# Block 0's weight split, the row splits and the last norm in the output projection of a hybrid layer

## The chip, the cores and the metric

The kernel runs on one core of a Trainium2 chip. The metric is the device time of one execution in microseconds (us). The engines are TensorE (PE, with PEld for its weight loads), VectorE (DVE), ScalarE (ACT), GpSimd (POOL) and SyncE (SP, which here only issues DMA transfers). Each engine works through its own instruction queue; semaphores order them against each other.

## The reference, cut to what matters

One layer of a diffusion backbone on 1024 latent tokens and 256 context tokens of width 1024, all in fp32:

```python
y_m = mlstm_merge(hm, om, mlstm_norm[l])               # 4 heads x 128, chunkwise mLSTM
y_a = window_attention(q, k, v, k_ctx, v_ctx, sink)    # 8 query / 2 kv heads x 64, |i-j| <= 128
x = x + g_a * (jnp.concatenate([y_m, y_a], axis=-1) @ w_out[l])
h = modulate(rmsnorm(x, norm_ffn[l]), sh_f, sc_f)
a, val = jnp.split(h @ w_up[l], 2, axis=-1)            # w_up: 1024 x 5632
x = x + g_f * ((gelu(dwconv(a, conv_w, conv_b)) * val) @ w_down[l])
return rmsnorm(x, final_norm)
```

## The kernel before, in words

Every fp32 matrix product is made of three products of fp32r halves: a value is split into a high half (a rounding copy) and a low half (value minus high half), and hi*hi, hi*lo and lo*hi are accumulated (`mm3`, lines 307 to 309). So each operand costs one cast and one subtraction before PE can use it; each product costs three PE instructions.

The stage that the change touches lies between attention and the up-projection. The tokens are eight tiles of 128 rows.

*Attention* (`Pair`, loop over `t`) runs 32 pairs of heads as a software pipeline: scores (`S`), row maximum, exponential (`ex`), scaling on POOL (`nrm`), transposes (`tr`), their splits (`hi` on ACT, `lo` on DVE), products with v (`pv`) into one PSUM tile `u` and the write of the result into `yTa` (`y1`, `y2`). `fill(t, i)` inserts other work at fixed places of a step: the mLSTM half of the output projection (`Wout(b, 0)`), the whole projection of tile 0 (`f0`), and row splits (`ysplit_h`, `ysplit_l`) of attention's result for the first tiles of the next loop. Steps are numbered up to n + 1, with n = 32.

*Output projection* (the loop over `order` = 4, 1, 5, 2, 6, 3, 7, from line 1471 on). For each tile b: two groups of twelve products (`wout_n(b, 0)`, `wout_n(b, 1)`) into two PSUM buffers (`po`), each added to the rows `xs[b]` on DVE (line 1374); sums of squares on ACT (`sq`); the norm factor (root on ACT, reciprocal on DVE) and the normed rows `hn` on ACT (`norm_b`); eight transposes on PE (`trans`); evacuation with scale and shift, four parts on ACT and four on DVE (`evac`, L1417 and L1419); and splits into `hB` (`split`, L1430 and L1192). These follow one another over three turns of the loop, so a turn works on the products of tile b, the norm of the tile before and the evacuation of the one before that.

*The up-projection is a Strassen product.* Tokens are two halves (tiles 0 to 3 and 4 to 7), so `hB` holds seven operands: B11, B21, B22 and the sums T1 to T4, which need both tiles of a pair (b - 4 and b; `sum1` to `sum4`). The weights come in pairs `Ra`, `Rb` with four sums (`sums_v`, `sums_g`) and splits (`wsplit`). Block 0's first product uses the weights `er`, split into `e0`. Its products a (with e0) start before the last tile is ready, on 384 of 512 columns; then come the groups f, c, b, e and d, and then block 1.

*What sets the order.* Attention and the loop over `order` are each written in a hand-ordered section (`manual_schedule`): PE, DVE, ACT and POOL take their instructions in program order there. What stands between or behind these sections (the split of `e0` at line 1349, the sums and splits from line 1571 on) and SP's queue are placed by the framework's planner. `held` is a list of postponed subtractions that `run` empties.

Of the kernel before, what the change touches and what calls it, by code (L numbers as in the profile page):

```python
# [9 lines left out]
F32 = mybir.dt.float32  # L10
F32R = mybir.dt.float32r
# [7 lines left out]
P = 128  # L19
# [59 lines left out]
def build(tc, I, out, dbg=None):  # L79
# [959 lines left out]


    p2 = ExitStack()
    yp = p2.enter_context(tc.tile_pool(name="yp", bufs=1))
    yTa = yp.tile([P, 4, SEQ], F32, name="yTa")
    wop = p2.enter_context(tc.tile_pool(name="wop", bufs=1))
    pb_ = ExitStack()
    t3 = pb_.enter_context(tc.tile_pool(name="t3", bufs=2, reuse_waits="tile"))
# [8 lines left out]
    class Wout:  # L1055
# [15 lines left out]
        def hi(self):  # L1071
            self.h, self.l = (t2.tile([P, 512], F32R, name=n, tag=n, bufs=1) for n in ("ymh", "yml"))
            r = lambda a: a[:].rearrange("p (j q) -> p j q", j=4)
            self.src = yTa[:, :, self.b * P:self.b * P + P] if self.attn else r(self.po)
            S.copy(r(self.h), self.src)

        def lo(self):
# [16 lines left out]
    class Pair:  # L1094
# [87 lines left out]

        def y2(self):
            u, ut = self.u, self.ut
            yf = yTa[:, 2 * self.g + self.r, self.b * P:(self.b + 1) * P]
            V.tensor_tensor(out=yf[0:64], in0=u[0:64, 0:P], in1=ut[0:64], op=ALU.add)
            V.tensor_tensor(out=yf[64:128], in0=u[64:128, P:2 * P], in1=ut[64:128], op=ALU.add)

    order = [4, 1, 5, 2, 6, 3, 7]
    ys = {}  # L1190
    yslice = lambda b: yTa[:, :, b * P:(b + 1) * P]
    sub = lambda e, o, x, y: e.tensor_tensor(out=o, in0=x, in1=y, op=ALU.subtract)  # L1192

    def ysplit_h(b, eng=G):
        ys[b] = [t4.tile([P, 4, P], F32R, name=f"y{n}", tag=f"y{n}", bufs=3 if n == "h" else 2) for n in "hl"]
        eng.copy(ys[b][0][:], yslice(b)) if eng is S else eng.tensor_copy(ys[b][0][:], yslice(b))

    def ysplit_l(b):
        sub(V, ys[b][1][:], yslice(b), ys[b][0][:].bitcast(F32))

    pairs = [(b, g, r) for b in range(NL) for g in range(KVH) for r in range(2)]
    pSs = [(pk, "pp")]
# [40 lines left out]
    more[n - 4, 0] += [f0.load]  # L1243
    more[n - 3, 2] += [f0.hi, f0.lo]
    tail_of(f0, n - 2)
    more[n - 5, 0] += [lambda: ysplit_h(order[0], S)]
    more[n - 5, 2] += [lambda: ysplit_l(order[0])]
    more[n - 4, 0] += [lambda: ysplit_h(order[1], S)]
    more[n - 3, 0] += [lambda: ysplit_l(order[1])]
    more[n - 2, 0] += [lambda: ysplit_h(order[2], S)]  # L1250

    attn = tc.manual_schedule(engines={mybir.EngineType.PE, mybir.EngineType.DVE, mybir.EngineType.Activation,
                                       mybir.EngineType.Pool})
# [86 lines left out]
    def split2(hi, lo, src):  # L1340
        S.copy(hi, src)
        V.tensor_tensor(out=lo, in0=src, in1=hi.bitcast(F32), op=ALU.subtract)  # L1342

    er = eW.tile([P, 2, 512], F32, name="er")
    e0 = [eW.tile([P, 2, 512], F32R, name=f"e0{n}") for n in "hl"]
    ar0 = eW.tile([P, 512], F32, name="ar0")
    a0 = [eW.tile([P, 512], F32R, name=f"a0{n}") for n in "hl"]
    nc.sync.dma_start(er[:], I["w_up"][0, :, 0:2].rearrange("p q k f -> p q (k f)"))
    split2(e0[0][:], e0[1][:], er[:])
    flat = lambda a: a[:].rearrange("p a b -> p (a b)")  # L1350

    pu = ExitStack()
# [9 lines left out]
    def load_x(b):  # L1362
        xs[b] = t3.tile([P, D], F32, name="x2", tag="x2")[:]
        nc.sync.dma_start(xs[b], x2_d[b][:])

    def wout_n(b, n, mid=None):
        ns = slice(512 * n, 512 * n + 512)
        po = pO.tile([P, 512], F32, name="po", tag="o")
        yh, yl = ys[b]
        for kt in range(4):  # L1370
            if kt == 2 and mid:
                mid()
            mm3(po[:], yh[:, kt], yl[:, kt], wos[4 + kt][0][:, ns], wos[4 + kt][1][:, ns], kt == 0, kt == 3)
        return lambda: V.tensor_tensor(out=xs[b][:, ns], in0=po[:], in1=xs[b][:, ns], op=ALU.add)

    def sq(b, n):
        if n == 0:
            hns[b] = t5.tile([P, D], F32, name="hn", tag="hn")
            rs[b] = t5.tile([P, 3], F32, name="r2", tag="r2")
        ns = slice(512 * n, 512 * n + 512)  # L1380
        S.activation(hns[b][:, ns], xs[b][:, ns], AF.Square, accum_out=rs[b][:, n:n + 1])
        if n == 1:
            run(1)
            V.tensor_scalar(out=rs[b][:, 2:3], in0=rs[b][:, 0:1], scalar1=1.0 / D, scalar2=EPS, op0=ALU.mult, op1=ALU.add)
            S.activation(rs[b][:, 0:1], rs[b][:, 1:2], AF.Sqrt, bias=rs[b][:, 2:3], scale=1.0 / D)
# [49 lines left out]
        sub(V, raws[b - 4][:, 0], raws[b][:, 0], raws[b - 4][:, 0])  # L1435

    def sum2(b):
        tbs[b] = tbp.tile([P, 1, 4, P], F32, name="tb", tag="tb", bufs=1)
        sub(V, tbs[b][:, 0], raws[b][:, 1], raws[b - 4][:, 0])

    def sum3(b, e=V):
# [13 lines left out]
    def prod(ps, wt, j, blk, first, last, by_part=None, cols=slice(0, 512), kts=range(4)):  # L1455
        seq = [(kt, p_) for p_ in by_part for kt in kts] if by_part else [(kt, p_) for kt in kts for p_ in parts]
        for n, (kt, (sw, part)) in enumerate(seq):
            T.matmul(ps[:, cols], wt[sw][:, j, kt * P:kt * P + P], hB[part][:, blk, kt, cols],  # L1458
                     start=first and n == 0, stop=last and n == len(seq) - 1,
                     skip_group_check=not first and len(kts) == 4)  # L1460

    load_x(order[0])
    fence = tc.manual_schedule(engines={mybir.EngineType.PE, mybir.EngineType.DVE, mybir.EngineType.Activation,
                                        mybir.EngineType.Pool})
# [6 lines left out]
    for i, b in enumerate(order):  # L1471
        prev = order[i - 1] if i else None
        pp = order[i - 2] if i > 1 else 0 if i == 1 else None
        add0 = wout_n(b, 0)
        if prev is not None:
            sq(prev, 1)
            norm_b(prev)
        run()
        if pp is not None:
            evac(pp)  # L1480
        if 0 < i and i + 2 < len(order):
            ysplit_h(order[i + 2])
        if 0 < i and i + 1 < len(order):
            ysplit_l(order[i + 1])
        if pp is not None and pp >= 4:
            held.append(split_b(pp))
        add0()
        sq(b, 0)
        if pp is not None and pp < 4:
            held.append(split(pp, B11, 2, raws[pp][:], V))  # L1490
            if late is not None:
                held.append(split_t3(late))
                held.append(split_t4(late))
            late = None
            run(1)
        if pp is not None and pp >= 4:
            sum1(pp)
            sum2(pp)
            held.append(split_t1(pp))
            held.append(split_t2(pp))  # L1500
            run(2)
            held += [lambda a=pp: sum3(a), lambda a=pp: sum4(a)]
            late = pp
        if b != last:
            add1 = wout_n(b, 1)
            trans(prev if i else 0)
            add1()
            nc.sync.dma_start(x2_d[b][:], xs[b])
# [12 lines left out]
    prod(ps_a2, e0, 1, B21, True, False, None, c3, range(2))
    trans(last, (4, 5, 6, 7))
    prod(ps_a2, e0, 1, B21, False, True, None, c3, range(2, 4))
    trans(last, (0, 1, 2, 3))
    prod(ps_a, e0, 0, B11, True, True, None, c1)
# [5 lines left out]
    p2.close()  # L1531


    f = ExitStack()
    fr = f.enter_context(tc.tile_pool(name="fr", bufs=1, reuse_waits="tile"))
    fw = f.enter_context(tc.tile_pool(name="fw", bufs=5, reuse_waits="tile"))
    add = lambda e, o, x, y: e.tensor_tensor(out=o, in0=x, in1=y, op=ALU.add)


    def load_R(m, ts=(0, 1), R=None):  # L1540
        R = R or [fr.tile([P, 2 + 3 * t, 512], F32, name=f"R{'ab'[t]}", tag=f"R{t}") if t in ts else None for t in range(2)]
        for t in ts:
            R[t] = R[t] or fr.tile([P, 2 + 3 * t, 512], F32, name=f"R{'ab'[t]}", tag=f"R{t}")
            nc.sync.dma_start(R[t][:, 0:2], I["w_up"][m, :, 2 * t:2 * t + 2].rearrange("p q k f -> p q (k f)"))
        return R

    def sums_v(R, e=V):
        add(e, R[1][:, 2], R[1][:, 1], R[1][:, 0])
        sub(e, R[1][:, 3], R[1][:, 2], R[0][:, 0])


    def sums_g(R, e=V):
        sub(e, R[1][:, 4], R[0][:, 1], R[1][:, 3])
        sub(e, R[1][:, 1], R[0][:, 0], R[1][:, 1])

    def wsplit(R, n):
        return wsplit_h(R, n)()

# [9 lines left out]
        return lo  # L1568


    R = load_R(0)
    sums_v(R)
    evac(last, range(4, 8))
    sub(V, R[1][:, 4], R[0][:, 1], R[1][:, 3])
    lo_b = split_b(last)
    wB = wsplit_h(R, 3)
    evac(last, range(4))
    lo_b()
    wB = wB()
    sum1(last)  # L1580
    wS = wsplit_h(R, 1)
    lo_1 = split_t1(last)
    S.copy(ar0[:], ps_a[:])
    run()
    wS = wS()
    sum2(last)
    lo_1()
    sub(V, R[1][:, 1], R[0][:, 0], R[1][:, 1])
    lo_2 = split_t2(last)
    lo_2()  # L1590
    lo_3, lo_4 = split_t3(late), split_t4(late)
    wA = wsplit_h(R, 2)
    lo_3()
    sum3(last)
    wA = wA()
    lo_5 = split_t3(last)
    lo_5()
    lo_4()
    sum4(last)
    split_t4(last)()  # L1600
    pTk.close()
    pC = pu.enter_context(tc.tile_pool(name="pC", bufs=4, space=PSUM, side="right", reuse_waits="tile"))
# [120 lines left out]
    for i in range(1, NF):  # L1723
# [416 lines left out]
```

## Time and profile before

| | us |
|---|---|
| median of 3 runs (lowest, highest) | 1275.53 (1273.96, 1277.4) |
| the profiled execution | 1275.56 |
| its span | 1273.7 |
| PE busy in the span | 1239.2 |
| DVE busy | 972.1 |
| ACT busy | 639.5 |
| POOL busy | 187.5 |

The span runs from the first to the last instruction of the trace; 1.9 us lie around it. Times inside the trace count from the start of the span. A row of a timeline gives start, duration, engine, line of the kernel, operation, output and inputs; in brackets stands how long the engine had been idle and what ended that. `wh`, `wl` are weight halves, `yh`, `yl` the halves of attention's result, `x` the rows, `hn` the normed rows.

### The profile page before, as it was taken

The page shows a single profiled execution, that of the slowest core. Times are in us where ns is not written, and L with a number is a line of the kernel's source. Part 1 is how long each engine was busy: PE and PEld are TensorE (multiplying, and loading weights), DVE is VectorE, ACT ScalarE, POOL GpSimd, SP SyncE. Part 2 cuts the span into 40 slices and gives each one's busy share as a digit, 9 for nine tenths or more (in the row PEclk, how much of TensorE's full clock was granted, in tenths as well). Part 3 has the DMA queues.
Part 4 walks back from the last instruction along what each step waited for, and adds up shares of the span by engine and source line. Part 5 has one row for each costly group of instructions (what it writes and reads, how often), then busy time and mean ns, then how long its engine had stood idle before and what let it go on. Part 6 is the DMA issues. An engine that isn't in the chain of part 4 may idle for free.

```text
span 1273.7 us, 19249 instructions
## 1 busy us (share of the span) xinstructions
PE 1239.2 (97%) x7047; PEld 1062.8 (83%) x7047; DVE 972.1 (76%) x1689; ACT 639.5 (50%) x1311; POOL 187.5 (15%) x162
## 2 busy tenths in 40 slices
PE   6999999999999999999899999999999999999997
PEld 4799998999898888888788888888888888788886
DVE  4863687878787888786997877777777776867887
ACT  6732556464865777776844333333333333434435
POOL 1200000000001444221002321232231232001000
PEclk9999999999999999999999999999999999999999
DMA  9531444462355332112423322233322337975553
GB/s 357 184 125 35 142 130 144 117 177 84 84 174 160 131 111 89 62 39 102 156 74 111 120 100 92 108 108 108 108 99 91 108 117 268 344 255 179 193 197 134
DMA packets 90416, 175.64 MB, mean 138 GB/s; under 512 B 12938, under 2 KB 29522, under 8 KB 90322
## 3 DMA queue, kind: packets, MB, share of 16 engines
q1 hardware_dynamic: 90034, 173.63, 40.4%
q8 instruction: 56, 0.92, 0.3%
q10 hardware_dynamic: 288, 0.79, 0.2%
q14 instruction: 38, 0.31, 0.1%
HBM read 136.05 MB, written 38.33 MB: 137 GB/s over the span
## 4 chain that ended last, share of the span: by engine, by line
PE 81%; DVE 7%; DMA 4%; ACT 4%; issue 2%; SPq 1%; POOL 1%; ACTq 0%; DVEq 0%; POOLq 0%
PE pd L1979 14%; PE pa L1458 9%; PE pc L1458 9%; PE pp L588 7%; PE pe L1458 5%; PE pb L1458 4%; PE pd L1458 4%; PE u L1175 3%; PE pt L1152 2%; PE pv L307 2%; PE pv L309 2%; PE pv L308 2%; PE po L307 2%; PE po L308 1%; PE po L309 1%
## 5 line engine op out<-in xcount | busy, mean ns | idle before, releaser
L1563 ACT CAST wh<-Rb 128x1024 fp32r<-128x1024 f32 (+1 forms) x66 | 59.5, 904 | 143.5 <-PE pd L1458 77.1
L1979 PE MATMUL pd<-dh,al 128*128 128x512 f32 x296 | 115.4, 390 | 0.7 <-DVE al L1342 0.6
L1979 PE MATMUL pd<-dl,ah 128*128 128x512 f32 x296 | 115.2, 389 | 0.0
L1979 PE MATMUL pd<-dh,ah 128*128 128x512 f32 x296 | 115.2, 389 | 0.0
L1458 PE MATMUL pc<-hB,wh 128*128 128x512 f32 x344 | 105.6, 389 | 0.0
L1458 PE MATMUL pa<-hB,wh 128*128 128x512 f32 x336 | 103.7, 390 | 0.2 <-ACT sn L1641 0.2
L1192 DVE TENSOR_TENSOR wl<-Rb,wh 128x1024 fp32r<-128x1024 f32 (+1 forms) x66 | 68.9, 1045 | 39.2 <-ACT wh L1563 38.6
L1677 POOL TENSOR_TENSOR tt<-vt,tt 128x512 f32<-128x512 f32 x22 | 29.5, 1340 | 349.0 <-ACT tt L1671 349.0
L588 PE MATMUL pp<-hl,wh 128*128 128x512 f32 x256 | 79.4, 405 | 0.0
L307 PE MATMUL pv<-wh,hl 128*128 128x256 f32 x256 | 76.0, 297 | 0.5 <-ACT ym L601 0.5
L1458 PEld LDWEIGHTS pc<-hB,wh 128*128 128x128 f32 x344 | 64.5, 188 | 13.5
L1458 PEld LDWEIGHTS pa<-hB,wh 128*128 128x128 f32 x336 | 62.9, 188 | 14.1 <-ACT sn L1641 1.1
L309 PE MATMUL pv<-wh,hl 128*128 128x256 f32 x256 | 72.3, 283 | 0.0
L308 PE MATMUL pv<-wl,hl 128*128 128x256 f32 x256 | 72.3, 282 | 0.0
L1458 PE MATMUL pc<-hB,wl 128*128 128x512 f32 x172 | 66.4, 389 | 0.0
L1979 PEld LDWEIGHTS pd<-dh,al 128*128 128x128 f32 x296 | 55.5, 188 | 12.8 <-DVE al L1342 1.4
L1979 PEld LDWEIGHTS pd<-dl,ah 128*128 128x128 f32 x296 | 55.6, 188 | 11.9 <-DVE dl L1342 0.2
L1458 PE MATMUL pa<-hB,wl 128*128 128x512 f32 x168 | 65.4, 389 | 0.0
L1979 PEld LDWEIGHTS pd<-dh,ah 128*128 128x128 f32 x296 | 55.6, 188 | 11.6
L1159 ACT CAST ph<-pt 128x512 fp32r<-128x512 f32 (+1 forms) x88 | 46.2, 525 | 27.6 <-PE pt L1152 27.4
L1458 PE MATMUL pe<-hB,wh 128*128 128x512 f32 x176 | 54.4, 390 | 0.0
L1458 PE MATMUL pb<-hB,wh 128*128 128x512 f32 x176 | 54.2, 389 | 0.0
(1065 smaller groups left out, 3695.5 us busy)
## 6 DMA issues: line engine op xcount, KB each, us to landing
w<-in_w_ada_dram SPq DMA_DIRECT2D x64, 256.0 KB, 2.7
br<-in_w_down_dram SPq DMA_DIRECT2D x25, 512.0 KB, 5.5
Ra<-in_w_up_dram SPq DMA_DIRECT2D x22, 512.0 KB, 3.6
Rb<-in_w_up_dram SPq DMA_DIRECT2D x22, 512.0 KB, 3.5
ar<-act_s SPq DMA_DIRECT2D x44, 256.0 KB, 3.0
act_a<-tt SPq DMA_DIRECT2D x33, 256.0 KB, 2.0
act_s<-tt SPq DMA_DIRECT2D x33, 256.0 KB, 2.0
wr<-in_w_h_dram SPq DMA_DIRECT2D x16, 512.0 KB, 4.4
```

The costliest lines, as they stand in the source:

```text
L307: T.matmul(ps, st_hi, mv_hi, start=first, stop=False)
L308: T.matmul(ps, st_hi, mv_lo, start=False, stop=False)
L309: T.matmul(ps, st_lo, mv_hi, start=False, stop=last)
L588: T.matmul(pp[:, 512 * n:512 * n + 512], wkq[sw][:, kt, cs], hl[n][part][:, kt, :], start=kt == 0 and sw + part == 0, stop=kt == KT - 1 an ...
L1152: T.transpose(self.pt[i][:, (2 * kk + j) * P:(2 * kk + j + 1) * P], self.p[j][:, kb * P:(kb + 1) * P], ident[:])
L1159: S.copy(self.ph[i][:, :w], self.pt[i][:, :w])
L1175: T.matmul(self.u[:], vv[:, c, self.g], part[i][:, kk * 2 * P:(kk + 1) * 2 * P], start=kb + m == 0, stop=kb == last and m == 1)
L1192: sub = lambda e, o, x, y: e.tensor_tensor(out=o, in0=x, in1=y, op=ALU.subtract)
L1458: T.matmul(ps[:, cols], wt[sw][:, j, kt * P:kt * P + P], hB[part][:, blk, kt, cols], start=first and n == 0, stop=last and n == len(seq) - ...
L1563: S.copy(wt[0][:], src)
L1677: G.tensor_tensor(out=self.tt[:, h2_], in0=self.vt[:], in1=self.tt[:, h2_], op=ALU.mult)
L1979: T.matmul(ps[:], ac[sa][:, js], w[sw], start=first and n == 0, stop=last and n == 2, skip_group_check=not fresh)
```

## The change

Attention's result becomes three tiles instead of one (blocks 0 and 1, blocks 2 to 6, block 7), and their memory is later used for block weights: `Ra` in the first, `Rb` in the second, `ar0` in the third. The row splits of tiles 4 and 1 are placed in attention's last two steps (n and n + 1) instead of n - 5 to n - 3. The split of `e0` and the high halves of the five other tiles stand in the loop's first turn (one on ACT, four on POOL, with room in `hB` columns that only the last pair of tiles fills); their low halves stand in the first three turns. In the turns 0 and 1 the high half of an evacuated tile is cast on ACT, afterwards on DVE. The weights `Ra`, `Rb` are loaded in turn 2, two of their sums are formed in turn 4 and two in turn 6 (through `held`). Behind the loop, the squares and the norm of the last tile stand ahead of the split of tile 3, and the rest is reordered.

```diff
-    yTa = yp.tile([P, 4, SEQ], F32, name="yTa")
+    yTa = [yp.tile([P, w, 4, P], F32, name="yT", tag=f"yT{w}") for w in (2, 5, 1)]
...
-    more[n - 5, 0] += [lambda: ysplit_h(order[0], S)]
-    more[n - 5, 2] += [lambda: ysplit_l(order[0])]
-    more[n - 4, 0] += [lambda: ysplit_h(order[1], S)]
-    more[n - 3, 0] += [lambda: ysplit_l(order[1])]
-    more[n - 2, 0] += [lambda: ysplit_h(order[2], S)]
+    more[n, 0] += [lambda: ysplit_h(order[0], S)]
+    more[n, 2] += [lambda: ysplit_l(order[0])]
+    more[n + 1, 0] += [lambda: ysplit_h(order[1], S)]
+    more[n + 1, 2] += [lambda: ysplit_l(order[1])]
...
-    split2(e0[0][:], e0[1][:], er[:])
...
-        if 0 < i and i + 2 < len(order):
-            ysplit_h(order[i + 2])
-        if 0 < i and i + 1 < len(order):
-            ysplit_l(order[i + 1])
-        if pp is not None and pp >= 4:
-            held.append(split_b(pp))
         add0()
+        if i == 0:
+            split2(e0[0][:], e0[1][:], er[:])
+            for j in range(2, 7):
+                ysplit_h(order[j], S if j == 2 else G, [hB[n][:, B22 + j - 2, :, 3 * P:4 * P] for n in range(2)])
         sq(b, 0)
+        for j in ((2, 3), (4, 5), (6,))[i] if i < 3 else ():
+            ysplit_l(order[j])
+        if b == last:
+            break
         if pp is not None and pp < 4:
-            held.append(split(pp, B11, 2, raws[pp][:], V))
+            held.append(split(pp, B11, 2, raws[pp][:], V if i > 1 else S))
...
+        if i == 2:
+            R = load_R(0)
+        if i == 3:
+            held.append(lambda: sums_v(R))
+        if i == 5:
+            held.append(lambda: (sub(V, R[1][:, 4], R[0][:, 1], R[1][:, 3]), sub(V, R[1][:, 1], R[0][:, 0], R[1][:, 1])))
...
     add1 = wout_n(last, 1, lambda: trans(prev))
     evac(prev)
     add1()
+    sum1(late)
+    sum2(late)
+    sq(last, 1)
+    lo_b = split_b(late)
+    norm_b(last, True)
     lo3 = split(prev, B11, 2, raws[prev][:])
-    sq(last, 1)
-    norm_b(last, True)
-    lo3()
+    lo_b()
     prod(ps_a, e0, 0, B11, True, True, None, c3)
     prod(ps_a2, e0, 1, B21, True, False, None, c3, range(2))
     trans(last, (4, 5, 6, 7))
+    evac(last, range(4, 8))
+    lo3()
...
-    R = load_R(0)
-    sums_v(R)
```

## Rows read from the trace of the kernel before

**Rows 1.** The page's first part: engine, busy us, share of the span, instructions.
```profile
PE 1239.2 (97%) x7047; PEld 1062.8 (83%) x7047; DVE 972.1 (76%) x1689; ACT 639.5 (50%) x1311; POOL 187.5 (15%) x162
```

**Rows 2.** Busy time by stage: stretch, length, engines (instructions), PE clock, DMA share, GB/s.
```profile
564.00:567.00 3.00, 1.42 (x9) 1.16 (x9) 1.88 (x4) 2.41 (x6) 0.20 (x1) 0.99 0.41 165
567.00:574.00 7.00, 6.79 (x26) 5.79 (x25) 4.46 (x10) 4.25 (x12) 1.80 (x3) 0.52 0.00 0
574.00:583.60 9.60, 9.16 (x59) 7.75 (x58) 5.02 (x10) 3.39 (x8) 0.93 (x2) 1.00 0.01 2
583.60:600.00 16.40, 16.40 (x83) 13.75 (x82) 9.97 (x25) 12.65 (x29) 1.54 (x2) 1.00 0.46 162
...
618.00:635.10 17.10, 14.09 (x71) 11.43 (x70) 16.04 (x36) 14.41 (x33) 0.00 (x0) 1.00 0.45 154
635.10:654.40 19.30, 18.55 (x98) 15.67 (x99) 18.24 (x30) 10.32 (x17) 0.00 (x0) 1.00 0.23 83
```

**Rows 3.** Timeline of the end of attention, PE, ACT and DVE.
```profile
564.55 0.47 PE L1175 MATMUL u<-ph,vv 128*128 128x256 f32 x2 [0.56 <-ACT p__7262 L1133]
...
564.86 0.40 PE L1175 MATMUL u<-pl__7266,vv 128*128 128x256 f32 x2
565.13 1.04 ACT L1341 CAST e0h<-er 128x1024 fp32r<-128x1024 f32 x1 [0.59 <-DMA er<-in_w_up_dram]
...
566.29 0.39 PE L1118 MATMUL sps<-kT,QT 128*128 128x256 f32 x1 [1.03 <-ACT sps L1109]
...
567.33 0.79 PE L1175 MATMUL u<-ph,vv 128*128 128x256 f32 x2 [0.21 <-ACT ph L1159]
```

**Rows 4.** Timeline of PE up to the first product of the output projection.
```profile
573.19 0.63 PE L308 MATMUL po<-wol,ymh 128*128 128x512 f32 x1
...
574.85 0.27 PE L1152 MATMUL pt<-ident,p__7262 128*128 128x128 f32 x1
...
583.62 0.39 PE L307 MATMUL po<-woh,yh 128*128 128x512 f32 x1
```

**Rows 5.** Timeline of PE in the output projection: instructions that follow a wait.
```profile
622.84 0.47 PE L307 MATMUL po<-woh,yh 128*128 128x512 f32 x1 [0.59 <-DVE x L1374]
...
627.72 1.09 PE L1406 MATMUL pt<-ident,hn 128*128 128x128 f32 x8 [0.52 <-ACT hn L1394]
...
635.85 0.66 PE L1406 MATMUL pt<-ident,hn 128*128 128x128 f32 x4 [2.52 <-DVE hn L1392]
```

**Rows 6.** Timeline of DVE in the output projection: tile 4's additions, one later turn.
```profile
587.60 0.69 DVE L1374 TENSOR_TENSOR x<-po,x 128x512 f32<-128x512 f32 x1
589.29 0.69 DVE L1374 TENSOR_TENSOR x<-po,x 128x512 f32<-128x512 f32 x1 [1.00 <-PE po L309]
...
622.01 0.68 DVE L1374 TENSOR_TENSOR x<-po,x 128x512 f32<-128x512 f32 x1
622.61 0.68 DVE L1430 CAST hB<-raw 128x1024 fp32r<-128x1024 f32 x1
623.32 1.22 DVE L1192 TENSOR_TENSOR hB<-raw,hB 128x1024 fp32r<-128x1024 f32 x1
624.47 0.68 DVE L1374 TENSOR_TENSOR x<-po,x 128x512 f32<-128x512 f32 x1
```

**Rows 7.** Timeline of ACT in the output projection: norm, evacuation, casts.
```profile
591.30 1.15 ACT L1394 ACTIVATE hn<-x,r 128x1024 f32<-128x1024 f32 x1 [0.23 <-DVE r L1389]
592.35 1.48 ACT L1417 ACTIVATE raw<-pt,ada 128x128 f32<-128x128 f32 x4
...
623.35 1.13 ACT L1430 CAST hB<-raw 128x512 fp32r<-128x512 f32 x2
```

**Rows 8.** POOL's casts of yh: ns shortest/median/longest, first and last start, forms.
```profile
L1196 POOL CAST yh<-yTa x4: 610/771/1106, 589.1 to 608.1; 128x512 fp32r<-128x512 f32 x4
```

**Rows 9.** The page's DMA issues: KB each, median us to landing.
```profile
Rb<-in_w_up_dram SPq DMA_DIRECT2D x22, 512.0 KB, 3.5
```

**Rows 10.** Timeline of DVE: the last norm's reciprocal and the last low half of T3.
```profile
635.11 0.16 DVE L1389 RECIPROCAL r<-r 128x1 f32<-128x1 f32 x1 [0.26 <-ACT r L1385]
...
648.35 0.68 DVE L1192 TENSOR_TENSOR hB<-er,hB 128x512 fp32r<-128x512 f32 x1
```

**Rows 11.** Timeline of PE: start of group f, and of block 1 behind group d.
```profile
640.46 2.04 PE L1458 MATMUL pf<-hB,wh 128*128 128x512 f32 x8
...
654.44 0.62 PE L1458 MATMUL pa<-hB,wh 128*128 128x512 f32 x2
```

More of the change, by code (lines that the diff above doesn't have):

```diff
@@ L1041, in build @@
     p2 = ExitStack()
-    yp = p2.enter_context(tc.tile_pool(name="yp", bufs=1))
-    yTa = yp.tile([P, 4, SEQ], F32, name="yTa")
+    yk = ExitStack()
+    yp = yk.enter_context(tc.tile_pool(name="yp", bufs=1))
+    yTa = [yp.tile([P, w, 4, P], F32, name="yT", tag=f"yT{w}") for w in (2, 5, 1)]
+    yslice = lambda b: yTa[0][:, b] if b < 2 else yTa[1][:, b - 2] if b < 7 else yTa[2][:, 0]
     wop = p2.enter_context(tc.tile_pool(name="wop", bufs=1))
@@ L1073, in hi @@
             r = lambda a: a[:].rearrange("p (j q) -> p j q", j=4)
-            self.src = yTa[:, :, self.b * P:self.b * P + P] if self.attn else r(self.po)
+            self.src = yslice(self.b) if self.attn else r(self.po)
             S.copy(r(self.h), self.src)
@@ L1184, in y2 @@
             u, ut = self.u, self.ut
-            yf = yTa[:, 2 * self.g + self.r, self.b * P:(self.b + 1) * P]
+            yf = yslice(self.b)[:, 2 * self.g + self.r]
             V.tensor_tensor(out=yf[0:64], in0=u[0:64, 0:P], in1=ut[0:64], op=ALU.add)
@@ L1190, in build, with ysplit_h @@
     ys = {}
-    yslice = lambda b: yTa[:, :, b * P:(b + 1) * P]
     sub = lambda e, o, x, y: e.tensor_tensor(out=o, in0=x, in1=y, op=ALU.subtract)
-    def ysplit_h(b, eng=G):
-        ys[b] = [t4.tile([P, 4, P], F32R, name=f"y{n}", tag=f"y{n}", bufs=3 if n == "h" else 2) for n in "hl"]
-        eng.copy(ys[b][0][:], yslice(b)) if eng is S else eng.tensor_copy(ys[b][0][:], yslice(b))
+    def ysplit_h(b, eng=G, room=None):
+        ys[b] = room or [t4.tile([P, 4, P], F32R, name=f"y{n}", tag=f"y{n}")[:] for n in "hl"]
+        eng.copy(ys[b][0], yslice(b)) if eng is S else eng.tensor_copy(ys[b][0], yslice(b))
     def ysplit_l(b):
-        sub(V, ys[b][1][:], yslice(b), ys[b][0][:].bitcast(F32))
+        sub(V, ys[b][1], yslice(b), ys[b][0].bitcast(F32))
     pairs = [(b, g, r) for b in range(NL) for g in range(KVH) for r in range(2)]
@@ L1345, in build @@
     e0 = [eW.tile([P, 2, 512], F32R, name=f"e0{n}") for n in "hl"]
-    ar0 = eW.tile([P, 512], F32, name="ar0")
     a0 = [eW.tile([P, 512], F32R, name=f"a0{n}") for n in "hl"]
     nc.sync.dma_start(er[:], I["w_up"][0, :, 0:2].rearrange("p q k f -> p q (k f)"))
-    split2(e0[0][:], e0[1][:], er[:])
     flat = lambda a: a[:].rearrange("p a b -> p (a b)")
@@ L1370, in wout_n @@
         for kt in range(4):
-            if kt == 2 and mid:
+            if kt == 3 and mid:
                 mid()
@@ L1437, in sum2 @@
     def sum2(b):
-        tbs[b] = tbp.tile([P, 1, 4, P], F32, name="tb", tag="tb", bufs=1)
+        tbs[b] = tbp.tile([P, 1, 4, P], F32, name="tb", tag="tb", bufs=2)
         sub(V, tbs[b][:, 0], raws[b][:, 1], raws[b - 4][:, 0])
@@ L1460, in prod, with load_R, sums_v, sums_g @@
                      skip_group_check=not first and len(kts) == 4)
+    add = lambda e, o, x, y: e.tensor_tensor(out=o, in0=x, in1=y, op=ALU.add)
+    def load_R(m, ts=(0, 1), R=None):
+        R = R or [None, None]
+        for t in ts:
+            R[t] = yp.tile([P, 2 + 3 * t, 512], F32, name=f"R{'ab'[t]}", tag=f"yT{2 + 3 * t}")
+            nc.sync.dma_start(R[t][:, 0:2], I["w_up"][m, :, 2 * t:2 * t + 2].rearrange("p q k f -> p q (k f)"))
+        return R
+    def sums_v(R, e=V):
+        add(e, R[1][:, 2], R[1][:, 1], R[1][:, 0])
+        sub(e, R[1][:, 3], R[1][:, 2], R[0][:, 0])
+    def sums_g(R, e=V):
+        sub(e, R[1][:, 4], R[0][:, 1], R[1][:, 3])
+        sub(e, R[1][:, 1], R[0][:, 0], R[1][:, 1])
     load_x(order[0])
@@ L1496, in build @@
         if pp is not None and pp >= 4:
+            held.append(split_b(pp))
             sum1(pp)
@@ L1503, in build @@
             late = pp
[L1504 to L1508, printed above, removed]
+        add1 = wout_n(b, 1)
+        trans(prev if i else 0)
+        add1()
+        nc.sync.dma_start(x2_d[b][:], xs[b])
         if i + 2 < len(order):
             load_x(order[i + 2])
+        if i == 2:
[4 more added lines that the diff above has]
+            held.append(lambda: (sub(V, R[1][:, 4], R[0][:, 1], R[1][:, 3]), sub(V, R[1][:, 1], R[0][:, 0], R[1][:, 1])))
+    late = pp
     ps_a, ps_a2 = (pA.tile([P, 512], F32, name="pa", tag="a") for _ in range(2))
@@ L1531, in build @@
     p2.close()
+    ar0 = yp.tile([P, 512], F32, name="ar0", tag="yT1")
     f = ExitStack()
-    fr = f.enter_context(tc.tile_pool(name="fr", bufs=1, reuse_waits="tile"))
     fw = f.enter_context(tc.tile_pool(name="fw", bufs=5, reuse_waits="tile"))
[L1537 to L1554, printed above, removed]
     def wsplit(R, n):
@@ L1568, in wsplit_h @@
         return lo
-    R = load_R(0)
-    sums_v(R)
-    evac(last, range(4, 8))
-    sub(V, R[1][:, 4], R[0][:, 1], R[1][:, 3])
     lo_b = split_b(last)
     wB = wsplit_h(R, 3)
+    lo_1 = split_t1(late)
     evac(last, range(4))
@@ L1579, in build @@
     wB = wB()
+    lo_1()
+    wS = wsplit_h(R, 1)
+    lo_2 = split_t2(late)
     sum1(last)
-    wS = wsplit_h(R, 1)
     lo_1 = split_t1(last)
-    S.copy(ar0[:], ps_a[:])
-    run()
     wS = wS()
+    lo_1()
+    lo_2()
+    sum4(late)
     sum2(last)
-    lo_1()
-    sub(V, R[1][:, 1], R[0][:, 0], R[1][:, 1])
     lo_2 = split_t2(last)
+    sum3(late)
     lo_2()
     lo_3, lo_4 = split_t3(late), split_t4(late)
+    S.copy(ar0[:], ps_a[:])
     wA = wsplit_h(R, 2)
+    sum3(last)
     lo_3()
-    sum3(last)
     wA = wA()
     lo_5 = split_t3(last)
+    sum4(last)
     lo_5()
     lo_4()
-    sum4(last)
     split_t4(last)()
@@ L1799, in build @@
     f.close()
+    yk.close()
     g = ExitStack()
```

## The prediction

> **What bounds the kernel now.** I read the page first: TensorE (PE) is busy 97% of the span [rows 1], so a change pays only where PE waits or runs at its lower clock. The table by stage then finds both around the edit [rows 2]. [...] In the output projection PE is full up to 618 and busy 14.09 of 17.10 us from there to 635.1, where VectorE (DVE) is busy 16.04: that end is paced by DVE. At its start (583.6 to 600) DVE is busy only 9.97 of 16.4. From 635.1 to 654.4 PE loses 0.75 more. All that this change could take back is therefore some 2 us of waits and 3.3 of low clock in attention's end, and 3.8 us (3.01 + 0.75) in and behind the projection.
>
> The timeline shows why. At 565.13 ScalarE (ACT), after 0.59 of idling for the load of er, casts e0h for 1.04; the sink copy that the next scores wait for stands behind it, and PE idles 1.03 [rows 3]. It had idled 0.56 before and idles 0.21 after, then the clock falls. A 512-column product then takes 0.63 where it takes 0.39 later [rows 4], start to start 0.43 against 0.23.
>
> Below, T is the time since the projection's first product, which stands at 583.62 in the trace [rows 4].
>
> **End of attention: e0 and the three early row splits leave.** Without e0h the sink copy follows the exponential at once, and the scores can start behind the product of 564.86 [rows 3], at 565.2. From there to the transposes of 574.85 [rows 4], PE's work at full clock is two score groups 1.15 (four products of 256 columns and a short one each), twelve products of 256 columns 1.4 (half of 0.23 each), eight transposes 0.9 (eight in 1.09, [rows 5]), six products of 512 columns 1.4: 4.8 us. DVE and ACT, laid out beside it, make PE wait about 0.45 for one low half (pl). So 574.85 comes at about 570.5, 4.3 us earlier. The wait of 0.56 at 564.55 stays: it ends with the pair before leaving its single PSUM buffer. The splits of tiles 4 and 1 return two pairs later, on ACT and DVE, which are busy 3.39 and 5.02 of the 9.6 us there [rows 2]. The cast holds back one ph cast by 0.52, which DVE's addition of po covers; without that cover it costs 0.5. Ends of this term: 1.2 us (waits of 1.03 and 0.21 go, the clock falls all the same) and 5.4 (the 0.56 and the 0.45 go as well). I take 4.3, since a busy PE at full clock is what both neighbouring rows of the table show.
>
> **Output projection, first three tiles.** Start to start, DVE needs 0.60 for 512 columns, 1.15 for a two-input 1024, 0.71 for a 1024 cast [rows 6]; ACT 1.05 for a norm, 1.4 for its half of an evacuation, 0.5 for a 512 cast (two in 1.13) [rows 7], 0.95 for a 1024 cast (1.04 long, [rows 3]). Both queues keep the written order. The norm of tile 0 starts on ACT at T 3.98, unchanged: its chain hangs on the end of attention. Behind it stand now e0h (T 5.0 to 6.1) and the high half of tile 5 (to 6.6). On DVE the first addition of tile 4 still starts at T 3.98 (587.60, [rows 6]); then e0l waits for e0h until 6.14, and with the low halves of tiles 5 and 2 DVE is engaged until 8.5. So tile 4's second addition starts at T 8.5, not at 5.67 (589.29, [rows 6]): 2.8 us later. PE does not feel it yet: the PSUM buffer that this frees is wanted at T 9.2, when it comes free.
>
> In tile 1 the whole chain behind that addition (square, root, norm, evacuation) is late by as much; the low halves of tiles 6 and 3 fill DVE, and the cast of tile 0's rows, now ACT's, ends at 14.6. DVE waits 1.2 for it, and the second addition starts at 15.8, not 12.2. PE wants that buffer at 15.7 and gets it at 16.6: 0.9 of waiting. From tile 2 on DVE no longer has low halves beyond one, nor the slowing by POOL's casts, which took between 0.61 and 1.11 us beside it [rows 8]; all four are now issued together behind attention, while DVE is mostly idle. The second additions come at T 22.9, 29.5, 37.2, 43.8 and 50.1; in the trace the last one is at 49.3. PE waits another 0.6, 0.1, 0.9 and 0.2 for buffers, which replaces the 0.59 [rows 5] and its like.
>
> **Weight sums.** Four DVE operations of 0.6 to 0.7 (2.5 us) move from behind the last norm into tiles 6 and 7. Their loads go on SP behind tile 6's rows, at about T 26, and land by T 30.6 at 3.5 us [rows 9] plus issue and rivalry with the row loads; the sums want them at T 31.4. Late by 1 us they stall DVE by 0.2, by 2 us 1.2. In exchange, five 0.6 operations of tile 6's sums and splits go behind the norm.
>
> **The last norm.** Its reciprocal comes at T 52.5, against 51.5 [rows 10]. PE, idle since 52.0, gets the transposes at T 53.2 (trace: 52.2 [rows 5]), so its idle shrinks from 2.52 to about 1.25. But the 1024 cast of tile 3's rows now stands behind the norm on ACT (to 54.6), its low half on DVE ends at T 55.9, and the products on the last 128 columns need it: they wait 0.85 and end at T 58.6, where the trace has 56.8 (640.46, [rows 11]). From the norm on, DVE must do 14.1 us of operations up to the last low half of T3, with 1.4 of waits for ACT, against 13.84 in all before (635.11 to 648.35 and 0.60 for that operation itself, [rows 10]). The fourth product group (e) wants that half at T 67.1 and gets it at 68.2: about 1.2 us. The five groups end at T 73.5; the trace has T 70.8 (654.44, [rows 11]). From there on PE is full before, and block 1's weights are ready 3 us before they are due.
>
> **The rest** costs nothing: the R tiles lie in y's memory, e0 and ar0 have other places, and all are free long before their next writer (covered by whole tiles of PE work; if not, a load of 3.5 is exposed).
>
> **Sum.** 4.3 earlier, 2.7 later: 1.6 us gained. The profiled execution took 1275.56 us for a span of 1273.7, the median is 1275.53; so 1274.0. The projection's term lies between -3.8 (all of PE's idle there goes) and +4.7 (the 2.8 of tile 4 is never caught up, and the 1.9 of the late products is added).
>
> **Rivals.** *The projection keeps pace:* DVE's idle at the start really takes the low halves, and the queue walk overrates ACT's holds. For it: DVE has 6.4 us idle there [rows 2]. Against: those low halves now stand behind an ACT cast that stands behind the norm. Then 4.3 remains and up to 3.8 is added: 1267.5 to 1271.2, middle 1269.5.
>
> *The low clock was not e0's:* the split goes, but the granted clock falls at the end of attention as before, since the 0.56 of idling and the short products stay. Then 1.2 is gained and 2.7 lost: 1277.0. Against: of the 1.80 us of idling that came ahead of the fall [rows 3], 0.56 is left.
>
> *The other side, slower:* the clock falls in the projection. PE now waits in nearly every tile for one of two PSUM buffers, and twice between transposes around the last norm. If it is granted half for a stretch like that of 567 to 574, this costs 3.3 us (6.79 of work at 0.48 less): 1277.3, and 1280.6 if it happens in tile 1 and again behind the norm; it decides from 1.6 us of lost work on. Against: after idling 2.52 us at 635.85 [rows 5] the clock stayed at 1.00 [rows 2]. [...] The trace's 0.59 wait on such a buffer, without a fall, speaks against it.
>
> **How the numbers follow.** About 0.3%, 3.8 us, is what a measurement of this kernel can tell from no change; that is 1271.7 and 1279.4. Forecast 0.50 (own range 1271.8 to 1276: two tenths each side of the walk's dozen waits); pace kept 0.26; low clock stays 0.13; falls in the projection 0.11. Faster gets 0.22 of the pace case and 0.04 of the forecast: 0.26. Slower gets 0.06 of the last case, 0.03 of the clock case with a late load, 0.01 of the forecast: 0.10. Same: 0.64. The range 1269.5 to 1277.8 leaves out half of the fastest case and the double fall.
>
> **What the changed profile would show.** Right: clock 1.00 throughout attention's end, the projection's first product 4 us earlier; then tile 4's second addition 8.5 us after it, ACT's cast in front of a DVE wait in tile 1, PE waits on x additions from tile 1 on, idle before the last transposes near 1.25, and the end of the fifth group near T 73.5. Wrong: a half clock anywhere from 560 to 660, or T 71 or less there.

## The result, and the profile after

The changed kernel takes 1279.79 us in the median (1277.65 to 1281.67), the kernel before, on the same chips, 1275.61: a ratio of 1.0027 with an interval of 1.0019 to 1.0035. It is slower by 4.2 us in the medians, 3.4 by the ratio, where 1274.0 was forecast. The profiled execution took 1280.79 us, 5.2 more than that of before, with a span of 1278.9.

The page's first part after, which answers to [rows 1]: all five sums are within 2 us of before, so it is not more work.

```profile
PE 1240.1 (97%) x7047; PEld 1062.2 (83%) x7047; DVE 970.5 (76%) x1688; ACT 640.6 (50%) x1312; POOL 186.8 (15%) x162
```

Busy time by stage after (columns as in [rows 2]; the last two rows are of the down projection):

```profile
566.00:573.00 7.00, 6.14 (x43) 5.47 (x44) 5.34 (x12) 5.36 (x15) 1.47 (x3) 1.00 0.00 0
573.00:581.50 8.50, 8.05 (x50) 6.65 (x48) 5.66 (x12) 4.42 (x10) 1.25 (x2) 1.00 0.01 2
...
616.00:633.00 17.00, 16.60 (x82) 13.64 (x82) 16.75 (x37) 13.81 (x33) 0.00 (x0) 1.00 0.39 142
633.00:652.40 19.40, 16.60 (x90) 13.88 (x89) 17.98 (x31) 12.62 (x22) 0.00 (x0) 1.00 0.15 55
1070.00:1080.00 10.00, 7.17 (x32) 5.62 (x30) 2.52 (x3) 1.36 (x2) 3.00 (x2) 0.97 0.70 236
1080.00:1090.00 10.00, 9.17 (x29) 6.91 (x30) 9.07 (x10) 4.75 (x6) 0.00 (x0) 0.69 1.05 389
```

The same two stretches of the down projection before:

```profile
1070.00:1080.00 10.00, 9.92 (x44) 7.88 (x43) 4.43 (x4) 3.36 (x4) 0.00 (x0) 1.00 0.99 341
1080.00:1090.00 10.00, 9.36 (x41) 7.29 (x41) 9.57 (x10) 4.92 (x5) 0.00 (x0) 1.00 1.05 387
```

Attention's end has lost its low clock (0.52 in [rows 2]). A new one stands 500 us later, where nothing was edited: 44 and 41 products became 32 and 29, or 24 too few at some 0.23 us each, 5.5 us. Reading only around the edit would have missed it.

The timeline of PE after answers to [rows 4, 5, 11]:

```profile
581.51 0.39 PE L307 MATMUL po<-woh,yh 128*128 128x512 f32 x1
...
605.06 0.50 PE L307 MATMUL po<-woh,hB 128*128 128x512 f32 x1 [0.48 <-DVE x L1372]
...
634.65 0.63 PE L1404 MATMUL pt<-ident,hn 128*128 128x128 f32 x4 [1.41 <-DVE hn L1390]
...
637.23 0.33 PE L1456 MATMUL pa<-hB,e0h 128*128 128x128 f32 x1 [0.40 <-DVE hB L1193]
...
639.85 2.07 PE L1456 MATMUL pf<-hB,wh 128*128 128x512 f32 x8
...
649.49 0.50 PE L1456 MATMUL pe<-hB,wh 128*128 128x512 f32 x1 [0.99 <-DVE hB L1193]
...
654.83 0.61 PE L1456 MATMUL pa<-hB,wh 128*128 128x512 f32 x2
...
1080.79 0.79 PE L1992 MATMUL pd<-dh,ah 128*128 128x512 f32 x1 [3.62 <-ACT ah L1341]
1081.38 0.63 PE L1992 MATMUL pd<-dl,ah 128*128 128x512 f32 x1
```

The timeline of DVE after, against [rows 6, 10]:

```profile
587.61 1.23 DVE L1342 TENSOR_TENSOR e0l<-er,e0h 128x1024 fp32r<-128x1024 f32 x1 [1.43 <-ACT e0h L1341]
589.96 0.68 DVE L1372 TENSOR_TENSOR x<-po,x 128x512 f32<-128x512 f32 x1
...
596.07 1.23 DVE L1193 TENSOR_TENSOR hB<-raw,hB 128x1024 fp32r<-128x1024 f32 x1 [1.07 <-ACT hB L1428]
597.21 0.68 DVE L1372 TENSOR_TENSOR x<-po,x 128x512 f32<-128x512 f32 x1
...
633.81 0.17 DVE L1387 RECIPROCAL r<-r 128x1 f32<-128x1 f32 x1 [0.42 <-ACT r L1383]
```

**The 5.2 us, stage by stage**, from PE's first products of each stage, before and after. Attention's first scores: 396.9 and 399.0, +2.1 for a part that the change leaves alone; over the twelve profiles of this study this point lies anywhere from 396.6 to 400.9, so it is scatter. From there to the projection's first product: 186.7 and 182.5, -4.2. From that to block 1: 70.8 and 73.3, +2.5. To the first product of the down projection (1055.2 and 1054.8): -0.8. From there to the end of the span: 218.5 and 224.1, +5.6. The first three terms behind the scatter were forecast, as -4.3, +2.7 and nothing. The last was forecast as nothing.

**Where the 5.6 begins.** SP's queue at the end of the up-projection, before and then after; `ae` are the down projection's early operands, `ar` later ones:

```profile
1048.41 0.89 SPq L1828 DMA_DIRECT2D ae<-act_a  x2
...
1052.42 0.79 SPq L1828 DMA_DIRECT2D ae<-act_a  x2
...
1062.50 0.88 SPq L1681 DMA_DIRECT2D act_a<-tt  x2
...
1069.54 0.96 SPq L1828 DMA_DIRECT2D ar<-act_a  x2
```
```profile
1055.03 0.98 SPq L1841 DMA_DIRECT2D ae<-act_a  x2
...
1056.53 0.94 SPq L1841 DMA_DIRECT2D ae<-act_a  x2
...
1066.92 0.88 SPq L1693 DMA_DIRECT2D act_a<-tt  x2
...
1073.96 0.96 SPq L1841 DMA_DIRECT2D ar<-act_a  x2
```

and what SP waited for there after (line, what it waited for: us, times, longest):

```profile
SPq L1841 <- PE pc L1456: 7.0, 1, 7.0
```

The first `ae` load waits 7.0 us for group c of the up-projection's last block. ACT after, in whose order the cast of `ae` stands ahead of the last gelu step (`tt`), and that ahead of the store which the `ar` load needs (`ah` and `al` are the halves of such an operand):

```profile
1058.61 1.05 ACT L1341 CAST ah<-ae 128x1024 fp32r<-128x1024 f32 x1 [5.47 <-DMA ae<-act_a]
...
1064.12 1.06 ACT L1683 ACTIVATE tt<-tt 128x1024 f32<-128x1024 f32 x1 [0.24 <-DVE tt L1679]
...
1079.69 1.04 ACT L1341 CAST ah<-ar 128x1024 fp32r<-128x1024 f32 x1 [0.30 <-DMA ar<-act_a]
```

Each step of this chain is 4.4 us late: the cast of `ae` (1054.18 before), the store, the `ar` load, the cast of `ar` (1075.26 before). PE had 0.8 us to spare and idles 3.62; the granted clock falls within that time, at 1079.4, and is 0.50 until 1086.

**Why the load waits** is in the placing of tiles. The block weights R moved from a pool of 14 KB per partition into y's memory of 16 KB, so the weight halves behind them lie 2 KB higher. `ae1` stays at bytes 27,104 to 31,200. In the kernel before a buffer of `wh2` lay there, and the load went out at 1048.41 while PE was still at its last groups. Now the lower 2 KB are the second buffer of `wl1`, which the very last product group reads.

### The profile page after: what moved, and what is told of

Its sections match the earlier page's. It is cut to its first block, busy times and chain, and to the rows that moved or that the text cites. A ratio compares the mean times of both kernels' runs of the same rounds, so it can differ in the third digit from the quotient of the medians.

```text
span 1278.9 us, 19255 instructions
## 1 busy us (share of the span) xinstructions
PE 1240.1 (97%) x7047; PEld 1062.2 (83%) x7047; DVE 970.5 (76%) x1688; ACT 640.6 (50%) x1312; POOL 186.8 (15%) x162
## 4 chain that ended last, share of the span: by engine, by line
PE 78%; DVE 8%; ACT 6%; DMA 4%; issue 3%; POOL 1%; SPq 0%; ACTq 0%; DVEq 0%; POOLq 0%
PE pd L1992 15%; PE pa L1456 9%; PE pc L1456 9%; PE pp L588 6%; PE pe L1456 5%; PE pd L1456 5%; PE pb L1456 4%; PE u L1177 2%; PE pt L1154 2%; PE pv L307 2%; PE pv L309 2%; PE pv L308 2%; PE px L309 1%; DMA w<-in_w_ada_dram 1%; PE px L307 1%
```

## Experiments

Each time is a median beside the kernel before on the same chip (1275.6 to 1276.1 in these runs).

**1. The changed kernel with 2 KB of padding.**

```diff
+    gb.tile([P, 512], F32, name="pad")
```

> The changed kernel with 2 KB of unused memory per partition put first into the pool of the down projection's early operands, so that the operand tiles ae1 and ae2 lie over the same weight halves as in the kernel before, while all that the change moves stays. Theory (memory): the load of ae1 waits in the changed kernel for the last product group of the up-projection, because ae1 lies over a weight half (wl1, second buffer) that this group still reads; with the pad the two loads go out at about 1048 and 1052 instead of 1055.0 and 1056.5, the 3.62 us wait of PE at 1080.8 and the low clock (0.84, then 0.50) behind it are gone, and the time is 5 to 6 us below the changed kernel's: 1274 to 1275. Rival (the place in SP's queue, the release of a whole pool, or drift from the earlier stages): the loads leave when they do now and the time stays at 1279 to 1280.

Measured: 1274.24, ratio 0.9984 (0.9975 to 0.9992), 5.5 us below the changed kernel. SP and PE of this run:

```profile
1046.47 0.89 SPq L1842 DMA_DIRECT2D ae<-act_a  x2
...
1047.94 0.95 SPq L1842 DMA_DIRECT2D ae<-act_a  x2
```
```profile
1085.15 0.50 PE L1993 MATMUL pd<-dh,al 128*128 128x512 f32 x1 [0.63 <-DVE al L1342]
```

The loads go out early (the second at 1047.94, where about 1052 was expected), PE's longest wait at this place is 0.63, as in the kernel before (0.64), and the clock stays at 1.00. The tile holds no data: only the place of others changed. What is left of the change is worth 1.8 us in the medians, against the 1.6 forecast.

**2. The converse: the kernel before, with `ae1` placed over `wl1`.**

```diff
-    a1, a1h, a6, a1l, a7 = (single(dt, n) for dt, n in (..., (F32, "a7")))
+    a1, a1h, a6, a1l = (single(dt, n) for dt, n in (...))
...
+    a7 = single(F32, "a7")
```

> The kernel before with one edit: the tile a7 is allocated behind the two early operands ae1 and ae2 instead of ahead of them, so that ae1 lies 2 KB lower, over the second buffer of wl1, as in the changed kernel. Nothing of attention or the output projection differs. Theory (memory): the loads of ae1 and ae2 go out behind the up-projection's last product group, at about 1055 and 1056.5 instead of 1048.4 and 1052.4; PE waits about 3 us near 1084 for the cast ah, and the time is 5 to 6 us above the kernel before: 1281. Rival (the stall comes from something else that the change did): the loads leave at 1048, the time is 1275 to 1276.

Measured: 1280.85, ratio 1.0037 (1.0023 to 1.0051), 4.8 us more.

```profile
1055.79 0.80 SPq L1829 DMA_DIRECT2D ae<-act_a  x2
```
```profile
1081.29 0.50 PE L1980 MATMUL pd<-dh,ah 128*128 128x512 f32 x1 [3.59 <-ACT ah L1341]
```

The late load, the 3.6 us wait and the clock of 0.50 behind it are there, in a program that differs from before in the place of three tiles. With experiment 1 this settles the cause: SP's order and the earlier stages are out.

**3. The kernel before with only the split of e0 moved** into the loop's first turn.

```diff
-    split2(e0[0][:], e0[1][:], er[:])
...
         add0()
+        if i == 0:
+            split2(e0[0][:], e0[1][:], er[:])
```

> The kernel before with only the split of e0 moved, from attention's end into the first turn of the loop over tiles, behind the first addition; row splits, memory and weight sums stay as before. Theory (e0's cast caused PE's idle time of 1.03 and the low clock after it): the projection's first product comes at 579.4 to 580.2 instead of 583.6, with the granted clock at 1.00 from 564 on; the projection loses 0.5 to 1.6 us of that again since e0's cast and subtraction (1.04 and 1.2) stand in its first turn; the time is 1272 to 1273.5. Rival (the early row splits had to leave too, or the clock falls in any case): first product at 582.5 or later, the granted clock near 0.5 in a stretch before it, time 1275 to 1277.

Measured: 1275.45, ratio 0.9995 (0.9986 to 1.0003): above what the theory expected, though its first half held. The first product comes 183.0 us behind the first scores (before 186.7), with the clock at 1.00. Then 3.2 us go again up to group f (T 60.1 against 56.8): 1.6 up to the last addition (T 50.9 against 49.3), the rest behind the last norm. PE there:

```profile
634.67 0.73 PE L1405 MATMUL pt<-ident,hn 128*128 128x128 f32 x4 [2.51 <-DVE hn L1391]
```
```profile
632.00:634.60 2.60, 0.16 (x1) 0.00 (x0) 2.31 (x7) 2.34 (x5) 0.00 (x0) 1.00 0.00 0
634.60:638.50 3.90, 3.83 (x17) 3.74 (x18) 3.87 (x8) 1.75 (x5) 0.00 (x0) 0.57 0.34 134
```

The idle time is that of [rows 5] (2.52), but here the granted clock fell to 0.57 behind it: 3.9 us at 0.43 less, which is 1.7 us of work. That low clock was not expected; it is what the prediction's slower rival feared, in a kernel without the early norm.

**4. The padded kernel with e0's split put back** to attention's end.

```diff
+    split2(e0[0][:], e0[1][:], er[:])
...
-        if i == 0:
-            split2(e0[0][:], e0[1][:], er[:])
```

> The changed kernel with the pad, and with one edit of the change undone: the split of e0 stands where it stood before, at the end of attention; the row splits of the first three tiles stay late, as in the changed kernel. Theory (the cast of e0h alone made PE idle 1.03 and the low clock that followed; moving it gave 3.7 of the 4.2 us in the run that moved it alone): the wait of about 1 us near 566 and a granted clock near 0.5 behind it are back, the projection's first product comes 3 to 4.2 us later than in the padded kernel, and the projection wins 1.2 to 1.5 us of that back, since DVE no longer waits 1.43 for e0h; time 1276 to 1277.5. Rival (the late row splits protect attention's end, so that e0 has room there): first product within 1.5 us of the padded kernel's, time 1273 to 1274.5.

Measured: 1273.17, ratio 0.9980 (0.9971 to 0.9989). The theory fell: the first product comes after 182.9 us, nearly as early as with e0 moved (182.5). Only its last part held: without e0h in DVE's way block 1 comes at T 71.8, 1.5 us sooner than in the padded kernel (73.3). But the rival's reason is not the whole of it either, since SP and ACT show that the cast is not where it was:

```profile
543.66 0.33 SPq L1347 DMA_DIRECT2D er<-in_w_up_dram  x1
```
```profile
547.54 1.05 ACT L1341 CAST e0h<-er 128x1024 fp32r<-128x1024 f32 x1
```

Before, er was loaded at 560.61, behind a wait of 20.6 us on PE, and cast at 565.13 [rows 3]. The reason is again a place in memory. The tile ar0 left the pool of er (2 KB), so er starts at 212,960 and not at 210,912; up to 212,960 lies `wrm`, weights of the mLSTM half that PE reads until 560.

**5. That placing alone, in the kernel before.**

```diff
+    ar0 = eW.tile([P, 512], F32, name="ar0")
     er = eW.tile([P, 2, 512], F32, name="er")
     e0 = [eW.tile([P, 2, 512], F32R, name=f"e0{n}") for n in "hl"]
-    ar0 = eW.tile([P, 512], F32, name="ar0")
```

> The kernel before with one line moved: the 2 KB tile ar0 is allocated ahead of er instead of behind e0, so that er lies 2 KB higher. In the kernel before the lower 2 KB of er overlap a weight tile of the mLSTM half (wrm) that PE reads until its product of 560; in the changed kernel, where ar0 left this pool, they do not. No instruction is added, removed or moved by hand. Theory (the low clock at attention's end came from er's late load, not from e0's place in the program): er is loaded near 543.5 instead of 560.6, e0h is cast near 547, where nothing waits for it, the wait of 1.03 and the half clock are gone, the projection's first product comes at 579.5 to 580.5 instead of 583.6, and the projection keeps its pace; time 1271.5 to 1273 (1.6 more where the clock falls behind the last norm's wait of 2.5). Rival (the split of e0 or the early row splits must leave attention's end): first product at 583, time 1275 to 1276.

Measured: 1274.21, ratio 0.9990 (0.9979 to 1.0000). The load goes out at 542.73, but the cast keeps its place in ACT's order, 564.27, now without a wait for er. PE and the stretch behind it:

```profile
565.42 0.39 PE L1118 MATMUL sps<-kT,QT 128*128 128x256 f32 x1 [0.33 <-ACT sps L1109]
```
```profile
564.00:567.00 3.00, 2.02 (x11) 1.46 (x11) 2.58 (x4) 3.00 (x8) 0.01 (x1) 1.00 0.00 0
567.00:574.00 7.00, 6.56 (x43) 5.66 (x43) 4.49 (x12) 4.84 (x14) 2.72 (x4) 1.00 0.00 0
```

PE's wait shrinks from 1.03 to 0.33, the clock stays at 1.00, and the first product comes after 184.0 us: 2.7 of the 4.2 us, for one line that moves no instruction by hand. This profiled execution was the fastest of twelve (1272.61); in the medians 1.4 us are left, and the interval reaches 1.0000. So what led to the low clock was the wait for er together with the cast. The theory's place for the cast (547) was wrong, and its time too low by over a microsecond.

**6. The splits of the projection placed anew** (on the padded kernel): the high halves of e0 and of the five tiles on POOL ahead of the loop, two low halves into DVE's idle time there, the others spread, the casts of evacuated tiles on DVE.

```diff
+    G.tensor_copy(e0[0][:], er[:])
+    sub(V, e0[1][:], er[:], e0[0][:].bitcast(F32))
+    for j in range(2, 7):
+        ysplit_h(order[j], G, ...)
+    ysplit_l(order[2])
     norm_b(0)
```

> The changed kernel with the 2 KB pad, and with the splits in the projection placed anew: e0's high half and the five high halves of rows all on POOL ahead of the loop, e0's low half and that of tile 5 on DVE before the first addition where it idled 2 us, the others' low halves spread over the first three turns, and the casts of evacuated tiles always on DVE. Theory (the projection's loss of 2.5 us is DVE waiting on ACT casts, 1.43 for e0h and 1.07 for hB, with low halves in the way of tile 4's second addition): that addition starts some 5.7 us after the first projection product instead of 8.45, the fifth group ends 69.5 to 71 us after it instead of 73.3, and the time is 2 to 3.5 us below the padded kernel without this: 1271 to 1272. Rival (the pace is set by the sum of DVE's work, wherever the splits stand, or by POOL's casts slowing DVE): the fifth group ends at 73 or later, time as of the padded kernel.

Measured: 1271.38, ratio 0.9962 (0.9949 to 0.9976). Tile 4's second addition starts at T 5.7 (585.98, first product at 580.3), PE waits for no x addition any more, and block 1 starts at T 70.1 (padded: 73.3). So the loss of 2.5 us in the projection was not DVE's sum of work, which even grew (64.1 us busy up to block 1 in the padded kernel, 65.5 here), but where ACT's casts and the low halves stood in DVE's way. This kernel moves them all at once; by experiment 4, e0's split alone is 1.5 us of it.

**7 and 8. On this kernel, the weight sums, then the last norm, undone.** In 7 the four sums stand behind the norm again; in 8 tile 6's sums and splits stand ahead of it, and the order behind it is as in the kernel before.

```diff
-        if i == 3:
-            held.append(lambda: sums_v(R))
...
+    sums_v(R)
+    sub(V, R[1][:, 4], R[0][:, 1], R[1][:, 3])
     lo_b = split_b(last)
```
```diff
         if b == last:
+            held.append(split_b(pp))
+            sum1(pp)
+            sum2(pp)
...
             break
```

> The filled kernel (pad, splits placed anew) with the part on weight sums undone: the two weight tiles are loaded as early as in the changed kernel, but their four sums on DVE (0.6 each, 2.5 us) stand behind the last norm again. Theory (DVE has room for them in tiles 6 and 7, and none behind the norm, where it is the engine that sets groups f and e): the loop's end comes no earlier, or by at most 1.2 us, the first product of group f or of e waits 1.5 to 2.5 us more, and the time is 1.3 to 2.5 us above the filled kernel: 1272.7 to 1274. Rival (DVE paces the loop and what follows by one sum of work, so the place makes no difference): the last reciprocal comes 2.5 us earlier, and the time is within 0.5 us of the filled kernel's 1271.4.

> The filled kernel with the part on the last norm undone: tile 6's sums and splits and tile 3's split stand ahead of the last norm again, the order behind it as in the kernel before; weight sums stay in the middle tiles. Theory (the early norm is worth what it takes from PE's idle time ahead of the last transposes): PE idles 2.5 to 3.8 us there instead of 1.40, what follows is less loaded so that group e no longer waits its 0.98, and the time is 0.8 to 1.6 us above the filled kernel, and 1.6 us more if the granted clock falls behind that idle time as it did behind 2.51 us in the run that moved e0 alone: 1272.2 to 1274.5. Rival (DVE's sum of work up to group e is the same, so nothing is lost): within 0.5 us of 1271.4.

Measured: 1273.22 (0.9978, 0.9968 to 0.9988) and 1273.11 (0.9987, 0.9973 to 1.0000), each some 1.8 us above 1271.38 in the median. With the sums late the last reciprocal comes 1.2 us sooner, but from the last transposes on PE waits 3.8 us in all instead of 2.8, and block 1 starts at T 71.5 instead of 70.1. With the norm late:

```profile
633.32 0.63 PE L1404 MATMUL pt<-ident,hn 128*128 128x128 f32 x4 [3.73 <-DVE hn L1390]
```
```profile
633.30:640.00 6.70, 6.68 (x35) 6.60 (x35) 5.61 (x10) 4.80 (x10) 0.00 (x0) 0.60 0.20 78
640.00:644.00 4.00, 4.00 (x13) 3.32 (x13) 3.83 (x7) 3.04 (x5) 0.00 (x0) 0.50 0.00 0
```

The idle time is 3.73, then the clock falls for some 10 us, to 645. This profiled execution took 1276.97, others of this kernel as little as 1270.47, at a mean granted clock of 0.998 instead of 0.995: the size of the fall, or whether it comes, seems to differ from run to run. That the early norm is worth having is clear: ten of eleven runs without it lie above all six of experiment 6. For the early sums it is less sure: four of nine runs without them lie within those six.

**9. Group e's operands first** behind the last norm, its weight cast in ACT's idle time.

```diff
+    wA = wsplit_h(R, 2)
     lo_2()
-    sum4(late)
     sum2(last)
...
+    sum4(late)
+    lo_4 = split_t4(late)
```

> The filled kernel with the order behind the last norm changed: the weight cast for groups e and d goes into ACT's idle time of 2.88 us, and on DVE the operands of group e stand ahead of those that only group d needs. Theory (group e's wait of 0.98 is DVE's order, not its sum of work): the wait goes, group d's operands are still in time, time 0.7 to 1.0 us below the filled kernel: 1270.4 to 1270.7. Rival (the wait only moves to group b or d): within 0.3 us of 1271.4.

Measured: 1269.30, ratio 0.9956 (0.9944 to 0.9969). Of PE's waits from the projection to block 1, two are left (0.98 for group e is gone), and block 1 starts at T 68.8 instead of 70.1; the median fell by 2.1 us, and what exceeds the 1.3 is within the scatter.

```profile
PE pt L1404 <- DVE hn L1390: 1.4, 1, 1.4
PE pa L1456 <- DVE hB L1193: 0.4, 1, 0.4
```

**10. The same with e0's split back at attention's end.**

> The kernel with the pad, the row splits placed anew and group e's operands first (1269.3), with e0's split put back to attention's end, where er now lands 17 us earlier. Theory (the place of e0 is worth nothing once er lands early and DVE has room in the first turns): within 0.7 us of 1269.3. Rival (POOL's cast of e0h and DVE's subtraction still cost the projection's start): 1 us or more faster, 1268 or less. Second rival (ACT is too full at attention's end): slower, 1270.5 or more.

Measured: 1270.09, ratio 0.9957 (0.9942 to 0.9972): no difference that can be told from 1269.30. Once er lands early and DVE has room, the place of e0 is worth nothing. Experiment 9's kernel is the best here, 6.6 us below the kernel before.

## Why the prediction was wrong

**The step that failed** is "The rest costs nothing: the R tiles lie in y's memory, e0 and ar0 have other places, and all are free long before their next writer". It asked when the moved tiles come free, and that held: R is loaded at 582 and 595 (even earlier than the T 26 of the prediction, which is 607), SP waits at most 1.3 us for y's tiles, and no engine waits for R. It did not ask what else shifts when a pool grows by 2 KB. The tile that stalled, `ae1`, is neither in the diff nor in the stage. Its price, 5.5 us by experiment 1, is larger than the whole forecast gain. The stage was left out because the views were read around the edit alone, and every rival lay in the projection or ahead of it, so 1279.8 was outside the range. That it lies near the prediction's two falls of the clock in the projection (1280.6) is chance.

**The steps that held.** Attention's end: 4.3 forecast, 4.2 found. Tile 4's second addition: T 8.5 and 8.45. Tile 1: DVE waits 1.2 forecast, 1.07 found, and its addition is at 15.8 and 15.7. The last reciprocal: T 52.5 and 52.3. PE's idle time ahead of the last transposes: 1.25 and 1.41, down from 2.52 [rows 5]. Late products: 0.85 and 0.40. Group f: T 58.6 and 58.3. Group e's wait: 1.2 and 0.99. Block 1: T 73.5 and 73.3. Walking the two queues by their rows was good to 0.3 us for the times within these 73 us; single waits were off by up to 0.45.

**Right for a reason that was incomplete.** The prediction laid the low clock to e0's cast. Moving the cast does remove it (experiment 3, 3.7 us). But the change also moves er's load 16 us ahead through ar0's place, and that alone gives 2.7 of the 4.2 us (experiment 5). The two overlap: with either alone the clock was 1.00 there. What the late row splits add to this was not tested alone.

**The rivals.** That the projection keeps pace did not happen, but could be made to (experiment 6). That the low clock was not e0's did not happen. The slower one, a fall of the clock in the projection, did not happen in the changed kernel: PE waited 0.63, 0.48 and 0.63 for a PSUM buffer, at 597.95, 605.06 and 616.18, and the clock was 1.00 from 560 to 655. These three short waits, 7 to 11 us apart, left it alone.

## What to carry to other kernels

When a change alters the size of a pool or moves a tile to another one, list what then lies over what, for every later tile that is loaded early, and look for the last reader of that memory; 2 KB cost 5.5 us in one place, and in another gave 2.7 us of a stage, of which the medians show 1.4. The load that waited for memory showed here as an SP wait on PE of 7.0 us, some 20 us ahead of the stall, and each step behind it in the fixed order of the queues, up to the cast that PE waited for, came 4.4 us late. Test it by a pad in the changed kernel and by the same overlap in the kernel before; both cost one line.

## What the runs showed of the hardware

The same idle time does not always end in the same clock. With 3.62 us (the changed kernel), 3.59 (experiment 2) and 3.73 (experiment 8) the granted clock fell to 0.50, in the first within the idle time, in the others behind it, and stayed there for some 7 us, 3 us and 10. Behind 2.51 it fell in one kernel (experiment 3), to 0.57 in the mean of 3.9 us; behind 2.52 (before) and 2.53 (experiment 5), both also ahead of the last transposes, it stayed at 1.00. Behind 1.40 or 1.41 it stayed at 1.00 in the five profiles that have such a wait there (the changed kernel and experiments 1, 6, 9 and 10). The longest idle time alone does not decide it either: at attention's end of the kernel before it fell to 0.50 at 566.97, behind 0.56 and 1.03 us and ahead of the 0.21 that the prediction counts among what came before the fall [rows 3]. Each of these is one profiled execution. Shortening an idle time can thus be worth more than its length: in experiment 3 the low clock behind the 2.51 us cost another 1.7 us of work.

Beside a cast on POOL some of DVE's operations took longer, a slowing that the prediction takes as gone from tile 2 on. In the kernel before, the 1024 cast of 608.34 took 0.92 us beside POOL's cast of 608.09, and 0.68 at 622.61 with POOL idle; two subtractions of 512 columns took 1.70 at 601.71 beside POOL's cast of 601.76, and 1.29 at 616.40 with POOL idle. The two-input 1024 of 594.65 took 1.23 beside POOL's cast of 595.42, and 1.22 at 623.32 with POOL idle.
